# A diffusion transformer layer on one core: modulation dots one by one through the first feed-forward half, GpSimd making the rests of the plain quarter-weights, earlier residual loads, and the filters' small network moved ahead of stage two

## The chip, the cores and the metric

The kernel runs on one core of one Trainium2 chip. The metric is the device time of one execution in microseconds (us), and the time of a version is the median of its runs. TensorE (PE in the profile, PEld for its weight loads), VectorE (DVE), ScalarE (ACT), GpSimd (POOL) and SyncE (SP) each run their own list of instructions in order. Most transfers are issued on SP's queue, and a few on GpSimd's.

## What is computed

One layer on 512 latent tokens and 256 context tokens of width 1024, all in fp32. This is the reference, cut to what matters here:

```python
m  = jnp.split(silu(c) @ mod_w + mod_b, 9);  mc = jnp.split(silu(c_ctx) @ mod_w + mod_b, 9)
h  = half_ffn(h,  m[0],  m[1],  m[2],  ffn_w_gate[0], ffn_w_up[0], ffn_w_down[0])   # hidden width 2816
hc = half_ffn(hc, mc[0], mc[1], mc[2], ffn_w_gate[0], ffn_w_up[0], ffn_w_down[0])
n  = modulate(rms_norm(h), m[3], m[4]);  nc = modulate(rms_norm(hc), mc[3], mc[4])
s_fw, s_bw = context_states(nc, ...)
out = token_mixers(n, s_fw, s_bw, hyena_kernels(...), ...)    # n @ w_in; HGRN2 heads; Hyena by FFT
h  = h + m[5] * out
h  = half_ffn(h, m[6], m[7], m[8], ffn_w_gate[1], ffn_w_up[1], ffn_w_down[1])
return rms_norm(h) * final_norm_w
# half_ffn(h) = h + 0.5 * gate * ((silu(x @ wg) * (x @ wu)) @ wd),  x = modulate(rms_norm(h), shift, scale)
```

`hyena_kernels` runs a small network on 512 positions (33 to 64 to 64 values, each layer followed by a sine) and multiplies its result with `hyena_w3`; the filters come out of that.

## The kernel before

Every fp32 product is made as three TensorE products of parts. ScalarE rounds an operand to its high part (`whi`), VectorE subtracts that from the operand to get the rest (`wlo`, line 143), and `mm3` (lines 316 to 319) adds high x high, low x high and high x low in PSUM. So each weight costs ScalarE and VectorE an instruction each before TensorE can use it.

**First feed-forward half (`ffn0`).** The 22 hidden blocks of 128 are worked in five groups, of 4, 4, 4, 4 and 6 blocks. A group makes gate and up products and then its part of the down product, in eight column blocks of 128 (`dm`). The down product's partial results are accumulated in DRAM (`y_dram`, `yc_dram`) and read back in the last group. Group 0 uses the plain form. In groups 1 to 4, two blocks are made together by a seven-product scheme: `quads0` cuts the two blocks' weights into quarters and yields seven quarter-weights of 128x512, of which three are plain quarters (a11, a12, a22) and four are sums (`qs`, line 250); `pair_products0` runs seven products of 12 matmuls over 386 columns (`product0`) and combines them. There are 18 calls of `quads0`: nine pairs of blocks, each for gate and for up. The plain quarters' rests come from a negated copy by ScalarE and an accumulating DMA from DRAM on GpSimd's queue; the rests of the sums come from VectorE.

**The modulation (`mod_steps`)** is a generator beside this work. It has 56 steps; each takes one 512 KB row of `mod_w` (`wmod`, loaded one step ahead into two buffers) and VectorE multiplies it with `silu(c)` and `silu(c_ctx)` and sums (line 392). The first 24 steps have a latent dot in two halves of 512 and a context dot of 1024; the other 32 have one of 1024. `adv(bg, n)` takes n steps. It is called once per pair of blocks and with n = 2 after each of a group's eight down columns.

**The token mixer (stage two)** has work of two kinds. Chains (context norm, filters, the convolutions in four channel blocks, the four heads) hang on one engine after the other. `fill` tiles (`ps_w`, 52 of them, 24 matmuls of 512 columns for most) are projections of the normed latents that nothing holds up. `Clock.run` puts them between the steps of a chain, which sets the order on each engine. `allowed` says which tiles may be taken: the z tiles (decays and queries of a head) not before the convolutions have begun. In a convolution `ps_e` is the forward transform and `ps_i` the inverse one.

**Buffers.** Tiles come from rotating pools: `c8` has 12 buffers of 8 KB per partition, `c4` 8, `c2` 15, `c1` 6, `quarters` 2, `wraw` 3, and `whi` and `wlo` 3 each. A load waits on SP's queue until its buffer is free, and what stands behind it on the queue waits as well.

Of the kernel before, what the change touches and what calls it, by code (L numbers as in the profile page):

```python
# [20 lines left out]
L = 512  # L21
# [74 lines left out]
def layer_kernel(ctx: ExitStack, tc: tile.TileContext, a: dict, out: bass.AP):  # L96
# [38 lines left out]
    def load(dst, src):  # L135
        nc.sync.dma_start(out=dst, in_=src)
# [15 lines left out]
    for g, (f0, f1) in enumerate(GROUPS0):  # L152
        if g == 0:
            gu = [(a[w][0, ft], 1024) for ft in range(f0, f1) for w in ("wg", "wu")]
            plan += hold(gu[:6], [RING] * 3 + [ONE8, RES2, TWO4]) + gu[6:]
        else:
            plan += [(a[w][0, ft], a[w][0, ft + 1], QUAD0) for ft in range(f0, f1, 2) for w in ("wg", "wu")]
        down = [(a["wd"][0, dm, :, f0 * P:f1 * P], (f1 - f0) * P) for dm in range(KT)]
        plan += hold(down, [RING] * 3 + [ONE8] * 3 + [RING] * 2) + down[0:3] if g == len(GROUPS0) - 1 else down
# [20 lines left out]
    def allowed(f):  # L180
        if f[0] == "z":
            return state["conv"] and f[1] - state["heads"] < 3
        if f[0] == "pb":
            return ("z", 3, 1) in state["done"] and state["heads"] > 1
        return True
# [53 lines left out]
    def quads0(src0, src1):  # L239


        raws = []
        for src in (src0, src1):
            raws.append(raw_tile("wraw"))
            load(raws[-1], src)
        (a11, a12), (a21, a22) = (r.rearrange("p (h c) -> h p c", h=2) for r in raws)

        def total(x, y):
            t = c2("qs", [512])
            V.tensor_tensor(out=t, in0=x, in1=y, op=ALU.add)  # L250
# [407 lines left out]
    prefetch(6)  # L658
# [12 lines left out]
    def filter_net():  # L671
        mf = c8("mf", [896])
        load(mf, a["masks"])
# [23 lines left out]
        PE.matmul(p1[:64, :], zw[0:EMB, 512:576], zw[0:EMB, 0:512], start=True, stop=True)  # L697
        h1 = zw[0:64, 1024:1536]
# [5 lines left out]
        h2 = zw[:, 1536:2048]  # L704
# [168 lines left out]
    def product0(name, x):  # L873
        whi, wlo, _ = weights()
        p_ = ps(name)
        for k in range(4):
            ks = slice(k * P, k * P + P)
            mm3([p_[:, 0:HW]], whi[:, ks], wlo[:, ks], [x[k]], k == 0, k == 3)
        return p_[:, 0:HW - 1]

    def pair_products0(name):
# [5 lines left out]
        V.tensor_tensor(out=u2, in0=product0("ps_p6", tsum[1]), in1=p1, op=ALU.add)  # L887
        A.copy(p7, product0("ps_p7", tsum[2]))
# [4 lines left out]
        V.tensor_tensor(out=res[:, 0, 0], in0=product0("ps_p2", [xone(4 + k, 0) for k in range(4)]), in1=p1, op=ALU.add)  # L893
        V.scalar_tensor_tensor(out=res[:, 1, 0], in0=product0("ps_p4", tsum[3]), scalar=-1.0, in1=res[:, 1, 0],
# [13 lines left out]
    bg = mod_steps()  # L908

    def ffn0():  # L910
        for gi, (f0, f1) in enumerate(GROUPS0):
            ml, mc = [], []
            if gi == 0:
# [51 lines left out]
            else:  # L965
                for ft in range(f0, f1, 2):
# [4 lines left out]
                    adv(bg)  # L971
# [11 lines left out]
            if gi < len(GROUPS0) - 1:  # L983
                for dm in range(KT):
# [12 lines left out]
            def residual0(h_, x_src, y_src, p_, m, dm, al, n):
                x, y = al("xr", [n]), al("yr", [n])
                load(x, x_src)
                load(y, y_src)  # L1000
                V.tensor_tensor(out=y, in0=p_, in1=y, op=ALU.add)
                V.scalar_tensor_tensor(out=h_, in0=y, scalar=m[:, 16 + dm:17 + dm], in1=x, op0=ALU.mult, op1=ALU.add)
# [6 lines left out]
            hc2 = c8("hc", [KT, C])  # L1009
            nhi, nlo = (Halves([c8(x, [4, L], F32R) for _ in range(2)]) for x in ("nhi", "nlo"))  # L1010
            for dm in range(KT):
# [3 lines left out]
                residual0(hk(hl2, dm), x0_dram[:, dm], y_dram[:, dm], pl, m_lat, dm, c2, L)  # L1015
# [4 lines left out]
            for n, dm in enumerate((6, 7, 3, 4, 5, 0, 1, 2)):  # L1020
# [5 lines left out]
                residual0(hc2[:, dm], a["ctxT"][:, dm], yc_dram[:, dm], pc[:, 0:C], m_ctx, dm, c1, C)  # L1026
# [25 lines left out]
    def fill_tile(f):  # L1052
# [63 lines left out]
        elif kind == "z":  # L1116
# [619 lines left out]
```

## Time and profile before

| | |
|---|---|
| median of 3 runs | 1676.86 us (1676.05 to 1678.73) |
| the profiled execution's time | 1675.28 us |
| its span in the trace | 1673.5 us |
| mean granted TensorE clock | 0.939 of full speed |
| busy: TensorE, VectorE | 89%, 69% of the span |
| busy: ScalarE, GpSimd | 40%, 26% of the span |

The profiled execution lies 1.6 us below the median. An engine's busy share is a mean over stages in which different things set the pace; a gap of TensorE costs its own length and sometimes a lower granted clock around it.

### The profile page before, as it was taken

Reading aid. Unit: us, or ns where it says so; the run is one execution under the profiler, and the core shown is the slowest. Engines: PE = TensorE matmul, PEld = TensorE weight load, DVE = VectorE, ACT = ScalarE, POOL = GpSimd, SP = SyncE. Lnnn points to the kernel's source line nnn. Section 1 sums busy time; section 2 is a strip of 40 time slices with the busy share of each in tenths; the row PEclk is TensorE's granted clock in tenths of the full one; section 3 lists DMA queues with packets and bytes.
Section 4 is the critical chain, followed back from the end, with each engine's and each line's share of the span. In section 5 each row is a group of like instructions: output and inputs, shape, how many; then the busy total and the mean of one; then the engine's idle time right before and its main releaser. Section 6 shows DMA issues by size and latency. Waiting matters only on the chain.

```text
span 1673.5 us, 22809 instructions
## 1 busy us (share of the span) xinstructions
PE 1489.9 (89%) x8560; PEld 1328.3 (79%) x8560; DVE 1150.2 (69%) x1814; ACT 670.9 (40%) x1196; POOL 429.3 (26%) x353
## 2 busy tenths in 40 slices
PE   8697698998999977999999438998989899999997
PEld 5596697998989966777777437887769898989897
DVE  7777776766836756654355896777755776959687
ACT  5352343444546524443233112335333433535353
POOL 1320224334343300003667401211233010202120
PEclk9899798999999998999999768999899999999999
DMA  7417649869595563334355312113243223232323
GB/s 308 157 51 239 178 106 235 231 173 269 149 195 117 125 199 117 125 119 157 97 166 180 129 56 74 63 51 114 76 154 105 70 82 103 88 114 95 107 78 93
DMA packets 92751, 223.77 MB, mean 134 GB/s; under 512 B 10396, under 2 KB 25504, under 8 KB 92257
## 3 DMA queue, kind: packets, MB, share of 16 engines
q1 hardware_dynamic: 75024, 193.18, 35.3%
q0 software_dynamic: 16032, 27.93, 9.3%
q8 instruction: 67, 1.10, 0.3%
q10 hardware_dynamic: 1584, 1.20, 0.2%
q14 instruction: 44, 0.35, 0.1%
HBM read 190.04 MB, written 32.24 MB: 133 GB/s over the span
## 4 chain that ended last, share of the span: by engine, by line
PE 62%; DVE 17%; DMA 11%; issue 5%; ACT 2%; POOL 2%; SPq 0%; ACTq 0%; DVEq 0%; POOLq 0%
PE ps_p L319 6%; PE ps_p L316 6%; PE ps_p L317 6%; PE ps_w L316 5%; PE ps_w L317 5%; PE ps_w L319 5%; DMA wmod<-in_mod_w 4%; PE ps_dl L316 3%; PE ps_dl L317 3%; PE ps_dl L319 3%; DVE x L1225 2%; DVE wlo L143 1%; DVE wmod L392 1%; PE ps_s L1362 1%; DMA yr<-y_dram 1%
## 5 line engine op out<-in xcount | busy, mean ns | idle before, releaser
L142 ACT CAST whi<-wraw 128x1024 fp32r<-128x1024 f32 (+2 forms) x160 | 134.5, 842 | 297.3 <-issue 88.2
L143 DVE TENSOR_TENSOR wlo<-wraw,whi 128x1024 fp32r<-128x1024 f32 (+2 forms) x111 | 114.1, 1031 | 88.6 <-ACT whi L142 86.5
L316 PE MATMUL ps_w<-nhi,whi 128*128 128x512 f32 x352 | 144.9, 412 | 0.0
L319 PE MATMUL ps_w<-nhi,wlo 128*128 128x512 f32 x352 | 141.0, 401 | 2.4 <-DVE wlo L143 2.4
L317 PE MATMUL ps_w<-nlo,whi 128*128 128x512 f32 x352 | 141.8, 403 | 0.0
L317 PE MATMUL ps_dl<-mid,whi 128*128 128x512 f32 (+1 forms) x318 | 122.5, 386 | 0.0
L319 PE MATMUL ps_dl<-mid,wlo 128*128 128x512 f32 (+1 forms) x318 | 122.2, 386 | 0.0
L316 PE MATMUL ps_dl<-mid,whi 128*128 128x512 f32 (+1 forms) x318 | 121.2, 388 | 0.0
L143 POOL TENSOR_TENSOR wlo<-wraw,whi 128x1024 fp32r<-128x1024 f32 x22 | 53.9, 2450 | 242.1 <-ACT whi L142 150.6
L1562 POOL TENSOR_TENSOR u<-p,res 128x512 f32<-128x512 f32 x18 | 33.0, 1832 | 284.5 <-ACT p L1557 140.8
L392 DVE SCALAR_TENSOR_TENSOR wmod<-wmod,cvb 128x1024 f32<-128x1024 f32 x56 | 68.6, 1229 | 31.4 <-DMA wmod<-in_mod_w 31.0
L316 PEld LDWEIGHTS ps_w<-nhi,whi 128*128 128x128 f32 x352 | 68.4, 194 | 17.1 <-issue 1.6
L319 PEld LDWEIGHTS ps_w<-nhi,wlo 128*128 128x128 f32 x352 | 67.9, 193 | 15.4 <-DVE wlo L143 2.8
L317 PEld LDWEIGHTS ps_w<-nlo,whi 128*128 128x128 f32 x352 | 68.2, 194 | 11.6
L142 ACT CAST wlo<-qs 128x512 fp32r<-128x512 f32 x72 | 43.7, 621 | 81.0 <-DVE qs L250 56.3
L319 PE MATMUL ps_p<-bh,whi 128*128 128x386 f32 x180 | 63.5, 354 | 8.9 <-DMA whi<-in_wg 5.7
L142 ACT CAST whi<-qs 128x512 fp32r<-128x512 f32 x72 | 44.1, 620 | 63.8 <-DVE qs L250 24.4
L316 PEld LDWEIGHTS ps_dl<-mid,whi 128*128 128x128 f32 x318 | 59.6, 188 | 11.8 <-ACT mid L142 0.2
L319 PEld LDWEIGHTS ps_dl<-mid,wlo 128*128 128x128 f32 x318 | 60.0, 189 | 7.1
L317 PEld LDWEIGHTS ps_dl<-mid,whi 128*128 128x128 f32 x318 | 59.8, 188 | 7.1
L143 DVE TENSOR_TENSOR wlo<-qs,wlo 128x512 fp32r<-128x512 f32 x72 | 54.9, 773 | 11.8 <-ACT wlo L142 11.5
L319 PE MATMUL ps_p<-bh,wlo 128*128 128x386 f32 x180 | 61.9, 344 | 1.1 <-DMA wlo<-in_wg 1.0
(541 smaller groups left out, 4923.7 us busy)
## 6 DMA issues: line engine op xcount, KB each, us to landing
wmod<-in_mod_w SPq DMA_DIRECT2D x56, 512.0 KB, 6.0
wraw<-in_wg SPq DMA_DIRECT2D x44, 512.0 KB, 4.1
wraw<-in_wu SPq DMA_DIRECT2D x44, 512.0 KB, 4.7
wraw<-in_w_in SPq DMA_DIRECT2D x44, 512.0 KB, 3.5
wraw<-in_wd SPq DMA_DIRECT2D x35, 384.0 KB, 3.6
wraw<-in_wd SPq DMA_DIRECT2D x40, 256.0 KB, 3.0
wm<-in_mod_w SPq DMA_DIRECT2D x16, 512.0 KB, 9.0
y_dram<-yt POOLq DMA_DIRECT2D x24, 256.0 KB, 8.1
```

The costliest lines, as they stand in the source:

```text
L142: A.copy(hi, x)
L143: return eng.tensor_tensor(out=lo, in0=x, in1=hi.bitcast(F32), op=ALU.subtract)
L316: PE.matmul(o, whi, xhi, start=first, stop=False)
L317: PE.matmul(o, whi, xlo, start=False, stop=False)
L319: PE.matmul(o, wlo, xhi, start=False, stop=last)
L392: return V.scalar_tensor_tensor(out=out_, in0=raw, scalar=1.0, in1=vec, op0=ALU.mult, op1=ALU.mult, accum_out=res)
L1225: V.tensor_tensor(out=r, in0=x, in1=y, op=op)
L1362: PE.matmul(p_[:, ss], km[:, ss], view(QA, c * P, ([2 * b, P // (2 * b)], [L + b, 2], [1, b])), start=True, stop=True)
L1562: G.tensor_tensor(out=u57, in0=p57, in1=res[:, 1:2].broadcast_to([P, 2, 256]), op=ALU.add)
```

## The change

The change has nine edits. (1) `adv(bg)` is called four times per pair of blocks (inside `pair_products0`) and once per down column, where it was once per pair and twice per column; so steps move from the downs into the products. (2) In `quads0` the rests of the three plain quarters are subtracted by GpSimd: 54 subtractions of 128x512 take the place of 54 negated copies on ScalarE and 54 accumulating DMAs. (3) `product0` fetches three weights ahead and not two. (4) In `residual0` of the last group, x and y of all column blocks are read at once into `c8` tiles ahead of the last down product, not per block through `c2` and `c1`. (5) `filter_net` runs behind `mod_steps` in the same background generator, with two `c4` tiles, and no longer at the start of `filters`. (6) Context norm and filters run as two chains side by side over the fill, and `forward_table` comes ahead of both. (7) Head 0's z tiles are allowed before the convolutions. (8) In `shifts`, at the start, the latent dots are made in two halves, and four of the eight rows are loaded ahead of the sixth kept weight. (9) Of the last down's kept weights one lies in a `quarters` buffer, not in `c8`.

```diff
@ plan, allowed
-        plan += hold(down, [RING] * 3 + [ONE8] * 3 + [RING] * 2) + down[0:3] if ...
+        plan += hold(down, [RING] * 3 + [ONE8] * 2 + [RES2] + [RING] * 2) + down[0:3] if ...
-            return state["conv"] and f[1] - state["heads"] < 3
+            return f[1] == 0 or (state["conv"] and f[1] - state["heads"] < 3)
@ quads0
-            if src is None:
-                split(t[:, 0], t[:, 1], x)
-            else:
-                A.copy(t[:, 0], x)
-                A.activation(t[:, 1], t[:, 0].bitcast(F32), AF.Copy, scale=-1.0)
-                nc.gpsimd.dma_start(out=t[:, 1], in_=src, accum_op=ALU.add)
+            split(t[:, 0], t[:, 1], x, eng)
-        yield both(a11, src0[:, 0:512])
+        yield both(a11, G)
...
-        yield both(a12, src0[:, 512:1024])
-        yield both(a22, src1[:, 512:1024])
+        yield both(a12, G)
+        yield both(a22, G)
@ shifts and its loads
-            dot(junk, shift_w[kt], cvb[0], m0[:, kt, 0:1])
+            junk = c2("junk", [512])
+            for h, res in enumerate((m0[:, kt, 0:1], m_part[:, kt:kt + 1])):
+                hs = slice(512 * h, 512 * h + 512)
+                dot(junk, shift_w[kt][:, hs], cvb[0][:, hs], res)
...
-    shift_w = rows(range(KT), "wm0")
+    shift_w = rows(range(4), "wm0")
+    prefetch(6)
+    shift_w += rows(range(4, KT), "wm0")
@ product0, pair_products0
-        whi, wlo, _ = weights()
+        whi, wlo, _ = weights(3)
...
         V.tensor_tensor(out=u2, in0=product0("ps_p6", tsum[1]), in1=p1, op=ALU.add)
+        adv(bg)
...
+        adv(bg)
@ ffn0
-                    adv(bg)
                     u_ = pair_products0("u")
...
-                    adv(bg, 2)
+                    adv(bg)
...
+            yl = [c8("yl", [4, L]) for _ in range(2)]
+            hc2, yc = (c8(x, [KT, C]) for x in ("hc", "yc"))
+            for dm in range(0, KT, 2):
+                i, ks = dm // 4, slice(dm % 4, dm % 4 + 2)
+                load(hl2[i][:, ks], x0_dram[:, dm:dm + 2])
+                load(yl[i][:, ks], y_dram[:, dm:dm + 2])
+            load(hc2, a["ctxT"])
+            load(yc, yc_dram)
@ background, filters, stage two
+    def background():
+        yield from mod_steps()
+        yield from filter_net()
...
-    ck.run([context_norm()], fill, lambda i: True)
     ftab = forward_table()
-    ck.run([filters()], fill, lambda i: True)
+    ck.run([context_norm(), filters()], fill, lambda i: True, 2)
```

How the instructions stand then, at three places. First VectorE between group 0's down product and group 1's first sum of quarters, in the kernel before: the last rows ahead of the first `qs`.

```order
L392 SCALAR_TENSOR_TENSOR wmod,m_ctx<-wmod,cvb 128x1024
L392 SCALAR_TENSOR_TENSOR junk,m_lat<-wmod,cvb 128x512
L392 SCALAR_TENSOR_TENSOR junk,m_part<-wmod,cvb 128x512
L392 SCALAR_TENSOR_TENSOR wmod,m_ctx<-wmod,cvb 128x1024
L392 SCALAR_TENSOR_TENSOR junk,m_lat<-wmod,cvb 128x512
L392 SCALAR_TENSOR_TENSOR junk,m_part<-wmod,cvb 128x512
L392 SCALAR_TENSOR_TENSOR wmod,m_ctx<-wmod,cvb 128x1024
L392 SCALAR_TENSOR_TENSOR junk,m_lat<-wmod,cvb 128x512
L250 TENSOR_TENSOR qs<-wraw 128x512
```

In the changed kernel the rows ahead of the same first `qs` are these (the dots' line is 386 there; `wlo<-wraw,whi` is the rest of a down weight).

```order
L143 TENSOR_TENSOR wlo<-wraw,whi 128x512
L386 SCALAR_TENSOR_TENSOR junk,m_part<-wmod,cvb 128x512
L386 SCALAR_TENSOR_TENSOR wmod,m_ctx<-wmod,cvb 128x1024
L386 SCALAR_TENSOR_TENSOR junk,m_lat<-wmod,cvb 128x512
L143 TENSOR_TENSOR wlo<-wraw,whi 128x512
L386 SCALAR_TENSOR_TENSOR junk,m_part<-wmod,cvb 128x512
L386 SCALAR_TENSOR_TENSOR wmod,m_ctx<-wmod,cvb 128x1024
L386 SCALAR_TENSOR_TENSOR junk,m_lat<-wmod,cvb 128x512
L386 SCALAR_TENSOR_TENSOR junk,m_part<-wmod,cvb 128x512
L386 SCALAR_TENSOR_TENSOR wmod,m_ctx<-wmod,cvb 128x1024
L386 SCALAR_TENSOR_TENSOR junk,m_lat<-wmod,cvb 128x512
L249 TENSOR_TENSOR qs<-wraw 128x512
```

The down weights' rests now stand among the dots up to shortly before the first `qs`, where before the last rows were dots alone; and 6 1/3 steps stand between the first dot and the first `qs`, where it was 13 1/3.

Second, TensorE in the first channel block of the convolutions, before: the inverse transform's first two matmuls stand right behind the forward transform's.

```order
L319 MATMUL ps_e<-zhi,ft 128x256
L316 MATMUL ps_e<-zhi,ft 128x256
L317 MATMUL ps_e<-zlo,ft 128x256
L319 MATMUL ps_e<-zhi,ft 128x256
L316 MATMUL ps_i<-ys,it 128x256 x2
L316 MATMUL ps_e<-zhi,ft 128x256
```

After: the same place, where five `ps_w` tiles stand between the two. The last of them ends here.

```order
L311 MATMUL ps_w<-nlo,whi 128x512
L313 MATMUL ps_w<-nhi,wlo 128x512
L310 MATMUL ps_w<-nhi,whi 128x512
L311 MATMUL ps_w<-nlo,whi 128x512
L313 MATMUL ps_w<-nhi,wlo 128x512
L310 MATMUL ps_i<-ys,it 128x256
L311 MATMUL ps_i<-ys,it 128x256
```

Ten such tiles, five and five, are now in the first two channel blocks; none was there before, and in the last two blocks there is none in either kernel.

Third, SP's queue around the last group's down product, before. `xr` and `yr` are a column block's residual and partial result, `wd` the down weights.

```order
L136 DMA wraw<-in_wd 128x768 x6
L136 DMA xr<-x_dram 128x512
L136 DMA yr<-y_dram 128x512
L139 DMA h_dram<-hl 128x512
L136 DMA xr<-x_dram 128x512
L136 DMA yr<-y_dram 128x512
L136 DMA wraw<-in_wd 128x768 x3
```

After:

```order
L136 DMA hl<-x_dram 128x1024
L136 DMA yl<-y_dram 128x1024
L136 DMA hl<-x_dram 128x1024
L136 DMA yl<-y_dram 128x1024
L136 DMA hl<-x_dram 128x1024
L136 DMA yl<-y_dram 128x1024
L136 DMA hl<-x_dram 128x1024
L136 DMA yl<-y_dram 128x1024
L136 DMA wraw<-in_wd 128x768
L136 DMA hc<-in_ctxT 128x2048
L136 DMA yc<-yc_dram 128x2048
L136 DMA wraw<-in_wd 128x768 x3
```

Before, the loads of x and y came block by block, the second pair behind the first store of `h_dram`; now the eight loads shown, of 512 KB each, stand behind the third down weight, two of 1 MB behind the fourth, and the stores of `h_dram` come after all of them.

## Rows read from the trace of the kernel before

**Rows 1.** The page: busy time, share of the span and instructions of each engine.
```profile
PE 1489.9 (89%) x8560; PEld 1328.3 (79%) x8560; DVE 1150.2 (69%) x1814; ACT 670.9 (40%) x1196; POOL 429.3 (26%) x353
```

**Rows 2.** TensorE's waits: us in total, times, longest.
```profile
PE ps_i L316 <- ACT ys L142: 40.4, 4, 22.2
PE ps_p L316 <- ACT wlo L142: 26.3, 4, 21.6
PE ps_sum L459 <- DVE acc L451: 20.6, 4, 13.4
```

**Rows 3.** Windows: us; PE, PEld, DVE, ACT, POOL busy; granted clock; DMA share; GB/s.
```profile
119.80:153.50 33.70, 33.70 (x194) 29.43 (x193) 25.29 (x57) 12.07 (x27) 0.91 (x1) 1.00 0.73 234
153.50:242.70 89.20, 64.05 (x339) 61.83 (x338) 68.23 (x135) 36.91 (x69) 22.77 (x23) 0.85 0.63 165
276.30:352.40 76.10, 66.79 (x340) 64.46 (x339) 57.67 (x100) 35.09 (x67) 25.67 (x26) 0.89 0.79 208
385.70:454.10 68.40, 62.83 (x338) 60.72 (x337) 52.10 (x80) 34.95 (x67) 25.37 (x25) 0.95 0.80 210
487.80:580.50 92.70, 89.97 (x507) 88.68 (x506) 59.43 (x86) 53.90 (x99) 36.24 (x37) 1.00 0.61 131
580.50:654.00 73.50, 57.22 (x317) 50.54 (x315) 43.84 (x65) 24.70 (x40) 3.58 (x2) 0.88 0.49 154
654.00:696.00 42.00, 34.38 (x138) 28.00 (x139) 25.60 (x47) 14.69 (x27) 0.00 (x0) 0.88 0.38 125
696.00:928.40 232.40, 232.40 (x1052) 182.00 (x1051) 119.78 (x137) 83.64 (x120) 103.75 (x95) 1.00 0.44 146
928.40:980.90 52.50, 12.08 (x76) 11.08 (x75) 49.49 (x82) 9.19 (x15) 14.67 (x13) 0.62 0.31 104
```

**Rows 4.** VectorE's dots, 153.5 to 242.7 us: busy us, mean ns, idle before.
```profile
L392 DVE SCALAR_TENSOR_TENSOR junk<-wmod,cvb 128x512 f32<-128x512 f32 x22 | 15.2, 690 | 3.7 <-DMA wmod<-in_mod_w 3.3
L392 DVE SCALAR_TENSOR_TENSOR wmod<-wmod,cvb 128x1024 f32<-128x1024 f32 x12 | 14.7, 1224 | 0.3
L392 DVE DVE_READ_ACCUMULATOR junk<-wmod,cvb 128x1 f32 x22 | 1.8, 83 | 0.0
```

**Rows 5.** Timeline of VectorE, then TensorE: start us, us, instruction [idle before].
```profile
127.89 0.68 DVE L392 SCALAR_TENSOR_TENSOR junk<-wmod,cvb 128x512 f32<-128x512 f32 x1
...
174.99 0.69 DVE L250 TENSOR_TENSOR qs<-wraw 128x512 f32<-128x512 f32 x1
...
177.60 0.69 PE L316 MATMUL ps_p<-tt,wlo 128*128 128x386 f32 x1 [21.62 <-ACT wlo L142]
```

**Rows 6.** VectorE's sums of quarters in group 4: busy us, mean ns, idle before.
```profile
L250 DVE TENSOR_TENSOR qs<-wraw 128x512 f32<-128x512 f32 x10 | 10.1, 1008 | 4.3 <-DMA wraw<-in_wu 4.3
L250 DVE TENSOR_TENSOR qs<-qs,wraw 128x512 f32<-128x512 f32 x5 | 7.2, 1431 | 0.2
L250 DVE TENSOR_TENSOR qs<-wraw,qs 128x512 f32<-128x512 f32 x6 | 4.1, 682 | 0.0
```

**Rows 7.** GpSimd, line 809: min/median/max ns, first and last start.
```profile
L809 POOL TENSOR_TENSOR te<-te x4: 1303/1523/2260, 798.5 to 930.5; 128x512 f32<-128x512 f32 x4
```

**Rows 8.** Timeline of TensorE in the last down product.
```profile
581.15 0.40 PE L316 MATMUL ps_dl<-mid,whi 128*128 128x512 f32 x1
581.38 0.39 PE L317 MATMUL ps_dl<-mid,whi 128*128 128x512 f32 x1
```

**Rows 9.** Timeline around the end of the last down's latent part.
```profile
631.26 1.87 PE L459 MATMUL ps_sum<-pick,acc 128*128 128x4 f32 x8 [13.42 <-DVE acc L451]
...
634.38 0.69 DVE L1001 TENSOR_TENSOR yr<-ps_dl,yr 128x512 f32<-128x512 f32 x1 [3.17 <-DMA yr<-y_dram]
```

**Rows 10.** Timeline of VectorE at the start, a shift dot.
```profile
50.23 1.22 DVE L392 SCALAR_TENSOR_TENSOR junk<-wm,cvb 128x1024 f32<-128x1024 f32 x1 [4.03 <-DMA wm<-in_mod_w]
```

**Rows 11.** The filter network's first operation, two layers: ns, starts.
```profile
L688 DVE TENSOR_SCALAR uk<-ps_f,sm x2: 794/798/802, 728.3 to 741.1; 64x512 f32<-64x512 f32 x1, 128x512 f32<-128x512 f32 x1
```

**Rows 12.** VectorE's rests of fill weights, 696.0 to 928.4 us.
```profile
L143 DVE TENSOR_TENSOR wlo<-wraw,whi 128x1024 fp32r<-128x1024 f32 x29 | 37.7, 1301 | 55.8 <-ACT whi L142 55.8
```

More of the change, by code (lines that the diff above doesn't have):

```diff
@@ L158, in layer_kernel @@
         down = [(a["wd"][0, dm, :, f0 * P:f1 * P], (f1 - f0) * P) for dm in range(KT)]
-        plan += hold(down, [RING] * 3 + [ONE8] * 3 + [RING] * 2) + down[0:3] if g == len(GROUPS0) - 1 else down
+        plan += hold(down, [RING] * 3 + [ONE8] * 2 + [RES2] + [RING] * 2) + down[0:3] if g == len(GROUPS0) - 1 else down
     plan += [None] * 52
@@ L251, in total, with both @@
             return t
-        def both(x, src=None):
+        def both(x, eng=V):
             w = ("whi", "wlo")[wstate["slot"]]
@@ L657, in layer_kernel @@
         first_norm(kt, 0, hl, rl[0], LATS, c2)
-    prefetch(6)
+    prefetch(5)
     cvb = [c4("cvb", [D]) for _ in range(2)]
@@ L661, in layer_kernel @@
         load(cvb[i], a["cvec"][:, i * D:i * D + D].partition_broadcast(P))
-    junk = c4("junk", [1024])
-    V.memset(junk[:, 0:1], 0.0)
-    shift_w = rows(range(KT), "wm0")
+    shift_w = rows(range(4), "wm0")
+    prefetch(6)
+    shift_w += rows(range(4, KT), "wm0")
     for i in range(2):
@@ L671, in filter_net @@
     def filter_net():
-        mf = c8("mf", [896])
-        load(mf, a["masks"])
+        za, zb = (c4("zw", [1024]) for _ in range(2))
+        load(za[:, 0:896], a["masks"])
         sm64 = c1("sm64", [132])
@@ L676, in filter_net @@
         yield
-        V.tensor_copy(masks.rearrange("p l s -> p (l s)"), mf)
+        V.tensor_copy(masks.rearrange("p l s -> p (l s)"), za[:, 0:896])
         yield
-        zw = c8("zw", [2048])
-        load(zw[0:EMB, 0:512], a["zT"])
-        load(zw[0:EMB, 512:576], a["hy_w1"])
+        load(za[0:EMB, 0:512], a["zT"])
+        load(za[0:EMB, 512:576], a["hy_w1"])
         yield
-        uk = c8("uk", [2, 512])
         def sine_layer(n, dst, p_, b, fr):
-            u, kk = uk[0:n, 0], uk[0:n, 1]
+            u, kk = za[0:n, 0:512], za[0:n, 512:1024]
             V.tensor_scalar(out=u, in0=p_[0:n, :], scalar1=b[0:n], scalar2=fr[0:n], op0=ALU.add, op1=ALU.mult)
@@ L696, in filter_net @@
         p1 = ps("ps_f1")
-        PE.matmul(p1[:64, :], zw[0:EMB, 512:576], zw[0:EMB, 0:512], start=True, stop=True)
-        h1 = zw[0:64, 1024:1536]
+        PE.matmul(p1[:64, :], za[0:EMB, 512:576], za[0:EMB, 0:512], start=True, stop=True)
+        h1 = zb[0:64, 0:512]
         sine_layer(64, h1, p1, sm64[:, 128:129], sm64[:, 129:130])
@@ L703, in filter_net @@
         PE.matmul(p2, sm64[0:64, 0:128], h1, start=True, stop=True)
-        h2 = zw[:, 1536:2048]
+        h2 = zb[:, 512:1024]
         sine_layer(P, h2, p2, sm64[:, 130:131], sm64[:, 131:132])
@@ L731, in filters @@
     def filters():
-        for _ in filter_net():
-            yield 0.4, 3.0
         worder = [(hh, q) for hh in range(2) for _ in range(2) for q in range(4)]
@@ L907, in layer_kernel @@
     n_c = 2 * (HC + 2)
-    bg = mod_steps()
+    def background():
+        yield from mod_steps()
+        yield from filter_net()
+    bg = background()
     def ffn0():
@@ L932, in ffn0 @@
                     first_norm(kt, 1, hc, rx[0], CTXS, c1)
+                V.tensor_tensor(out=m0[:, :, 0], in0=m0[:, :, 0], in1=m_part, op=ALU.add)
                 V.tensor_tensor(out=m0, in0=m0, in1=sm[:, S_MODB:S_MODB + KT].unsqueeze(2).broadcast_to([P, KT, 2]), op=ALU.add)
@@ L993, in ffn0, with residual0 @@
                             nc.gpsimd.dma_start(out=y[:, dm], in_=t, accum_op=ALU.add)
-                    adv(bg, 2)
+                    adv(bg)
                 continue
[L997 to L1000, printed above, removed]
+            def residual0(h_, y, p_, m, dm):
                 V.tensor_tensor(out=y, in0=p_, in1=y, op=ALU.add)
-                V.scalar_tensor_tensor(out=h_, in0=y, scalar=m[:, 16 + dm:17 + dm], in1=x, op0=ALU.mult, op1=ALU.add)
+                V.scalar_tensor_tensor(out=h_, in0=y, scalar=m[:, 16 + dm:17 + dm], in1=h_, op0=ALU.mult, op1=ALU.add)
             for _ in bg:
@@ L1008, in ffn0 @@
             hl2 = [c8("hl", [4, L]) for _ in range(2)]
-            hc2 = c8("hc", [KT, C])
+            yl = [c8("yl", [4, L]) for _ in range(2)]
[6 more added lines that the diff above has]
+            load(yc, yc_dram)
             nhi, nlo = (Halves([c8(x, [4, L], F32R) for _ in range(2)]) for x in ("nhi", "nlo"))
@@ L1014, in ffn0 @@
                 down(kept[dm], lx, [pl])
-                residual0(hk(hl2, dm), x0_dram[:, dm], y_dram[:, dm], pl, m_lat, dm, c2, L)
+                residual0(hk(hl2, dm), hk(yl, dm), pl, m_lat, dm)
                 sq_add(acc, hk(hl2, dm), dm, c2, L)
@@ L1025, in ffn0 @@
                     adv(nl, 1 if n < 3 else 2)
-                residual0(hc2[:, dm], a["ctxT"][:, dm], yc_dram[:, dm], pc[:, 0:C], m_ctx, dm, c1, C)
+                residual0(hc2[:, dm], yc[:, dm], pc[:, 0:C], m_ctx, dm)
                 sq_add(accc, hc2[:, dm], n, c1, C)
@@ L1124, in fill_tile @@
                 if d == 0:
-                    hs["F"] = c8("F", [2, T])
-                    hs["KR"] = c8("KR", [2, T])
+                    for k in ("F", "KR"):
+                        hs[k] = c8(k, [2, T]) if hd else \
+                            quarters(k).rearrange("p a b -> p (a b)")[:, 0:2 * T].rearrange("p (d t) -> p d t", d=2)
                 ci = slice(d * NH + hd, d * NH + hd + 1)
```

## The prediction, made before the changed kernel had run

> **What bounds the kernel now.** I read the page first. TensorE is busy for 1489.9 us of the span and VectorE for 1150.2 [rows 1], so what can be won is mostly TensorE's idle time, some 184 us, and what a lowered clock costs around it. The second view is TensorE's waits. The three that lead the list [rows 2] are the inverse transform waiting for its spectrum (40.4 us in four waits), a quarter-weight in the product stages (26.3, of which one wait is 21.6) and the sum of squares of the first half's result (20.6, of which one is 13.4). Each lies in one stage, so the third view is windows by stage [rows 3]. In their order they are group 0's down product, the products of groups 1, 2, 3 and 4, the last down product (latents, then context), the context norm, the filters with the fill, and the first two channel blocks of the convolutions.
>
> What the reader is to see there: group 0's down and the filters have TensorE busy throughout, so there only less TensorE work helps. Group 4 makes three pairs of blocks and no modulation dots in 92.7 us with TensorE busy for 89.97 at full clock: 30.9 us a pair. Groups 1 to 3 make two pairs each, which at that pace is 61.8, and take 89.2, 76.1 and 68.4, at granted clocks of 0.85, 0.89 and 0.95. The first two convolution blocks take 52.5 us with 12.08 of TensorE, at 0.62, while VectorE is busy for 49.49.
>
> **The change, term by term**, against the profiled execution's 1675.3 us, 1.6 below the median.
>
> *Product stages (edits 1, 2, 3).* A modulation step of the first kind costs VectorE two dots at 0.690, one at 1.224 and three reads of 0.083 us [rows 4], together 2.85; a later one 1.31. The first dot starts at 127.89 and group 1's first sum of quarters at 174.99; 13 1/3 steps stand between. TensorE, having waited 21.62 us, gets its first product at 177.60 [rows 5]. Now 6 1/3 steps stand there: 7 steps of 2.85 are 20 us of VectorE's queue, nearly the wait. They move behind that sum, into products. Is VectorE late there? Without dots, group 4 asks 59.43 / 3 = 19.8 us a pair of it [rows 3], so 39.6 for two pairs. Group 1's products now hold eight steps (22.8), those of groups 2 and 3 eight short ones (10.5).
>
> The rests come on top. No row shows GpSimd making one, but it makes sums of the same 128x512 tiles in 1.3 us at best and 1.523 in the median [rows 7]: I take 1.5. What does that take from VectorE? In group 4 its sums of two loaded quarters take 0.682 us undisturbed in one form, 1.008 and 1.431 in the others [rows 6], which is 7 us over 21 sums, and the rests of the sums lose some 2 us more. GpSimd was busy for 36.24 us there [rows 3], of which its DMA issues are about 16, so 20 with sums. That is 9.4 / 20, or 0.47 us lost per us of GpSimd's sums. A group of two pairs has 12 rests: 12 x 1.5 x 0.47 = 8.4 us. The bounds are nothing lost and the whole 1.5 us a rest.
>
> VectorE then needs 39.6 + 22.8 + 8.4 = 70.8 us in group 1 and 58.5 in groups 2 and 3, against TensorE's 61.8. I take 74 (VectorE's work and some waits), 64 and 64 (TensorE's pace and some waits). In group 4 VectorE has 59.4 + 12.6 + 7.5, under 92.7, so I take 93. The 7.5 is the filter network: two layers of six operations whose dearest takes 0.798 us [rows 11], so under 10 in any case. The sum is 295 against 326.4: **31 less**. Best case: no interference, 45 less (62, 62, 62 and 92.7 are 279, and a little of the downs). Worst case: the whole 1.5 us a rest (80, 68, 68 and 96 are 312, so 14 less) and 10 us of new waits: 4 less. The 54 copies on ScalarE and the accumulating DMAs that go cost nothing now, as ScalarE is busy for half or less of each window. The downs stay as they are: group 0's is TensorE's own 33.70, and one step a column leaves VectorE less work there, not more.
>
> The Trainium skill (SBUF — State Buffer, section "SBUF: two separate sides") speaks against edit 2: the port pair that VectorE and GpSimd share is an exclusive lock, so a VectorE operation with two SBUF inputs and a GpSimd operation that reads SBUF shut each other out for a whole instruction. By it each rest would take its full 1.5 us of VectorE, and the stages would come to 80 + 68 + 68 + 96 = 312, 14 less and not 31. The trace agrees in part: sums in SBUF take up to 1.431 where 0.682 would do [rows 6], but not each one.
>
> *Last down and context norm (edits 4, 9).* The down stage takes 73.5 us. A matmul of 512 columns starts every 0.23 us [rows 8]; 8 columns x 6 blocks x 3 of them are 33, and the context's, at half the columns, 17: TensorE's own part is 50. The last waits there are a y load that VectorE waits 3.17 us for and, behind it, a sum for which TensorE stood 13.42 us [rows 9]. The loads now go out before the down begins: 6 MB at the 234 GB/s of the fastest window [rows 3] are 26 us, and they can start some 8 us before the stage, when the buffers of the up product's operand sums come free (its last four products, 48 matmuls, follow). Behind them on SP wait four down weights, needed from 12 us into the stage on; the first latent columns may wait a little. Fill starts where the down ends, and edit 6 lets it start at once beside the norm. I put TensorE's restart at 55 us and not 73.5, and save 4 of the norm's own gaps: **22 less**. Bounds: 12 (the loads are late as before, only the sum's wait goes) and 27.
>
> *Filters and convolutions (edits 5, 6, 7).* Ten fill tiles move from the filters' stage into the first two convolution blocks. Each is 24 matmuls of 0.23, so 5.5 us. The filter stage is TensorE's own time throughout [rows 3], so it loses 55 us. Each tile also needs its weight's rest, 1.3 us of VectorE [rows 12]. In the convolution blocks TensorE then has 55 + 11, VectorE 49.5 + 13 = 62.5: I take 68.5 in place of 52.5, 16 more. **39 less**. Bounds: 25 (the two engines half in turn, 82.5) and 45 (VectorE's sum alone, with no wait). The last two blocks keep their waits, since no fill stands there.
>
> *Start (edit 8).* VectorE waits 4.03 us for a row before its first dots [rows 10]; half of the rows now go ahead of a 512 KB weight. Eight dots in halves cost 8 x (2 x 0.773 - 1.307) = 1.9 us more. **3 less**; bounds 6 less and 2 more.
>
> Sum: 31 + 22 + 39 + 3 = 95, so 1580 for the profiled execution and **1582** for the median.
>
> **The rivals.** *A, the products gain nothing:* VectorE loses so much to GpSimd that all 31 go, 0.58 us a rest beyond my price. For it speak the 1.431 in [rows 6], against it that TensorE has some slack in groups 2 to 4: 1613. By the page's lock alone it would be 1599. *B, the filters become the bound:* with 55 us of fill gone, norm and filters hold 209 us of TensorE work (232.4, and about 32 of the norm's 34.38 at full clock, less 55), but VectorE's 119.8 - 7.5 + 25.6 and GpSimd's 103.75 [rows 3] add to 242 if they run strictly in turn. Then 33 come back: 1615. Against it: GpSimd's sums of one filter can lie under VectorE's work on the next. *C, the early loads come late*, because the `c8` buffers come free late or the down weights queue behind 6 MB: the term falls to 4, and it ends at 1600. *D, slower:* GpSimd runs in order. A rest may stand behind a combining sum that waits for a later product, and TensorE, which needs that rest, waits in turn. From 95 / 54 = 1.8 us a rest it decides against the change; with 1.5 for the rest itself and 1.3 for one sum ahead of it, 2.8 each is 151 us: 1733. Against it: weights are now made three ahead.
>
> **How the numbers follow.** Forecast 0.62 (own range 1562 to 1600), A 0.14, B 0.12, C 0.05, D 0.04, and 0.03 for more gain than the bounds or no change at all. The range takes in A, B and C above, with some us of scatter, and reaches down to about where all the best bounds together would end (45 + 27 + 45 + 6 = 123 less, 1554): 1556 to 1622. It leaves out D and the tails. Within 0.2% is about what a measurement of this kernel can tell from no change; all cases but D and part of the last give faster: 0.94, same 0.02, slower 0.04.
>
> **What would show it.** Right: TensorE's gap before group 1 falls from 21.6 us to a few, groups 1 to 3 take about 74, 64 and 64 at a granted clock near 1, the wait for `acc` goes, `ps_w` matmuls fill the first two convolution blocks, and VectorE's 128x512 sums get longer. Wrong: GpSimd leads TensorE's waits in the products (A, D), TensorE idles among the filters (B), or VectorE waits for `yl` (C). I would be furthest off if a weight that now comes later on SP's queue held TensorE.

## The result and the profile after

The changed kernel takes 1597.85 us in the median (1596.63 to 1599.40, four runs), beside 1676.45 for the kernel before: a ratio of 0.9529, 95% interval 0.9513 to 0.9546. That is 78.6 us less, where 95 were forecast. The page of its profile begins so:

```profile
span 1597.4 us, 22680 instructions
...
PE 1473.6 (92%) x8560; PEld 1312.8 (82%) x8560; DVE 1190.6 (75%) x1833; ACT 634.5 (40%) x1141; POOL 473.4 (30%) x350
```

TensorE is busy for 16 us less than before [rows 1], so some 60 of the 76 us that the span lost were idle time. VectorE is busy for 40 us more, although hardly any of its work is new (the start's dots are made in halves). TensorE's waits (us in total, times, longest):

```profile
PE ps_j L310 <- ACT ys L142: 22.1, 3, 13.9
PE ps_gc L310 <- ACT bh L142: 18.2, 1, 18.2
PE ps_ot L1439 <- ACT on L1433: 11.6, 4, 3.2
PE ps_p L310 <- ACT wlo L142: 11.0, 1, 11.0
PE ps_p L313 <- DVE wlo L143: 8.4, 10, 1.4
PE ps_p L313 <- DVE whi L143: 7.1, 6, 2.3
PE ps_p L310 <- ACT whi L142: 6.6, 3, 2.8
```

Of the three waits that led before [rows 2], `ps_i` and `ps_sum` are gone from the top and the 21.6 us ahead of group 1 too. In the products four smaller ones stand in their place, 33.1 us together, one of them 11.0, and the start's wait has grown to 18.2. The windows by stage, with columns as in [rows 3], are in their order group 0's down, the products of groups 1 to 4, the last down, context norm and filters together, the first two convolution blocks, and the rest up to the projections behind the heads.

```profile
125.40:159.20 33.80, 33.80 (x195) 29.54 (x194) 27.11 (x59) 12.57 (x29) 1.30 (x1) 1.00 0.75 253
159.20:229.30 70.10, 61.32 (x338) 58.77 (x337) 70.00 (x108) 28.05 (x56) 34.98 (x23) 1.00 0.38 122
...
264.00:342.80 78.80, 63.38 (x339) 60.59 (x338) 70.67 (x103) 27.98 (x56) 36.29 (x25) 0.94 0.46 140
...
376.50:440.90 64.40, 61.46 (x338) 60.61 (x337) 56.16 (x73) 28.38 (x56) 36.97 (x25) 0.97 0.51 155
...
474.60:570.50 95.90, 93.11 (x510) 90.73 (x509) 79.65 (x110) 46.59 (x88) 49.45 (x38) 0.98 0.34 102
570.50:624.40 53.90, 53.48 (x314) 46.99 (x313) 40.43 (x61) 24.17 (x38) 2.76 (x2) 1.00 0.59 215
624.40:856.30 231.90, 226.64 (x1057) 179.98 (x1056) 136.78 (x173) 85.29 (x131) 95.85 (x92) 0.99 0.42 138
856.30:922.80 66.50, 66.50 (x326) 55.80 (x325) 60.01 (x91) 24.06 (x35) 18.08 (x15) 1.00 0.47 155
922.80:1149.80 227.00, 182.34 (x1113) 163.47 (x1111) 168.76 (x296) 85.84 (x173) 45.89 (x19) 0.90 0.26 89
```

Against the kernel before, by the spans of the two profiled executions (76.1 us in all): group 0's down begins 5.6 later; from there to the last down it is 460.7 before and 445.1 now, 15.6 less; last down, norm and filters take 347.9 and 285.8, 62.1 less; the first two convolution blocks 52.5 and 66.5, 14 more; blocks three and four and the heads 245.2 and 227.0, 18.2 less; the rest is the same within 0.2.

### The profile page after: what moved, and what is told of

Same layout as the page of the kernel before. It is cut to its first block, busy times and chain, and to the rows that moved or that the text cites. A ratio compares the mean times of both kernels' runs of the same rounds, so it can differ in the third digit from the quotient of the medians.

```text
span 1597.4 us, 22680 instructions
## 1 busy us (share of the span) xinstructions
PE 1473.6 (92%) x8560; PEld 1312.8 (82%) x8560; DVE 1190.6 (75%) x1833; ACT 634.5 (40%) x1141; POOL 473.4 (30%) x350
## 4 chain that ended last, share of the span: by engine, by line
PE 59%; DVE 22%; DMA 7%; issue 6%; ACT 3%; POOL 1%; SPq 0%; ACTq 0%; DVEq 0%; POOLq 0%
PE ps_w L310 5%; PE ps_w L313 5%; PE ps_w L311 5%; PE ps_p L313 4%; PE ps_p L310 4%; PE ps_p L311 4%; PE ps_dl L310 3%; PE ps_dl L311 3%; PE ps_dl L313 3%; DMA wmod<-in_mod_w 3%; DVE wlo L143 2%; DVE junk L386 2%; DVE wmod L386 2%; DVE qs L249 2%; DVE whi L143 2%
## 5 line engine op out<-in xcount | busy, mean ns | idle before, releaser
L142 ACT CAST whi<-wraw 128x512 fp32r<-128x512 f32 (+2 forms) x187 | 151.4, 810 | 299.1 <-issue 78.4
L143 DVE TENSOR_TENSOR wlo<-wraw,whi 128x1024 fp32r<-128x1024 f32 (+2 forms) x114 | 124.6, 1095 | 57.4 <-ACT whi L142 55.1
L386 DVE SCALAR_TENSOR_TENSOR wmod<-wmod,cvb 128x1024 f32<-128x1024 f32 x56 | 73.5, 1313 | 24.6 <-DMA wmod<-in_mod_w 24.3
L311 PEld LDWEIGHTS ps_w<-nlo,whi 128*128 128x128 f32 x352 | 67.2, 191 | 11.5
L142 ACT CAST whi<-qs 128x512 fp32r<-128x512 f32 x72 | 44.3, 619 | 78.8 <-DVE qs L249 40.2
L143 DVE TENSOR_TENSOR whi<-qs,whi 128x512 fp32r<-128x512 f32 x72 | 67.4, 947 | 4.6 <-ACT whi L142 4.3
L143 DVE TENSOR_TENSOR wlo<-qs,wlo 128x512 fp32r<-128x512 f32 x72 | 58.1, 813 | 16.6 <-ACT wlo L142 15.9
L143 POOL TENSOR_TENSOR wlo<-wraw,wlo 128x512 fp32r<-128x512 f32 x27 | 48.2, 1785 | 65.7 <-ACT wlo L142 58.3
```

The lines of the kernel that those rows point to most:

```text
L311: PE.matmul(o, whi, xlo, start=False, stop=False)
L386: return V.scalar_tensor_tensor(out=out_, in0=raw, scalar=1.0, in1=vec, op0=ALU.mult, op1=ALU.mult, accum_out=res)
```

## Experiments

The theory after this result: the stages of the mixer and the last down did what the prediction says, and the 16 us that are missing lie in the products, where GpSimd's rests (edit 2) take VectorE time just where the steps (edit 1) have been put, and at the start (edit 8). The rival: the rests are cheap, and the rows of `mod_w` or the pairs' weights are late. Every run was compared with runs of the kernel before on the same chip; the ratios are to that kernel, so 0.9529 is the changed kernel.

**1. The rests by copies and accumulating DMAs again (edit 2 undone): 1585.05 us, 0.9457 (0.9435 to 0.9479).**

```diff
-            split(t[:, 0], t[:, 1], x, eng)
+            if src is None:
+                split(t[:, 0], t[:, 1], x)
+            else:
+                A.copy(t[:, 0], x)
+                A.activation(t[:, 1], t[:, 0].bitcast(F32), AF.Copy, scale=-1.0)
+                nc.gpsimd.dma_start(out=t[:, 1], in_=src, accum_op=ALU.add)
...
-        yield both(a11, G)
+        yield both(a11, src0[:, 0:512])
...
```

> The changed kernel with edit 2 undone: the 54 rests come again from a negated copy on ScalarE and an accumulating DMA. If GpSimd's rests cost VectorE time that TensorE waits for (my price, 8.4 us a group, with group 1's VectorE now busy for 70.00 of 70.1 us), groups 1 and 2 get 6 to 8 us shorter each and the time is about 1585. If the rests are free and the accumulating DMAs are late beside the rows of mod_w, TensorE waits for them in the products and it is 1605 or more. Group 1's VectorE busy time tells which.

Windows of groups 1 and 2 in this run, and the wait that came back:

```profile
158.90:220.40 61.50, 60.08 (x338) 59.01 (x337) 59.95 (x109) 33.91 (x65) 25.42 (x23) 1.00 0.72 192
...
254.10:328.60 74.50, 64.63 (x338) 62.96 (x337) 59.19 (x108) 35.51 (x67) 25.70 (x25) 0.89 0.78 199
```

```profile
PE ps_p L318 <- DMA whi<-in_wg: 14.1, 4, 5.2
```

Edit 2 alone costs 13 us. Group 1's VectorE is busy for 59.95 us and not 70.00, and the stage takes 61.5 us and not 70.1; group 2 gains less than I expected, 4.3 us. The rival's wait for accumulating DMAs is there too (14.1 us), so this is not yet the best place for the rests. From group 0's down to the end of group 4's products (125 to 560 us) VectorE makes the same 573 instructions as in the changed kernel, whose line stands in the next experiment, in

```profile
125.00:560.00 435.00, 414.96 (x2290) 392.00 (x2289) 322.71 (x573) 210.80 (x410) 155.42 (x156) 0.97 0.76 201
```

322.71 us, where the changed kernel takes 366.08: 43.4 us more beside GpSimd's 54 rests, or 0.80 each.

**2. The rests on VectorE: 1569.20 us, 0.9358 (0.9339 to 0.9377).**

```diff
-        yield both(a11, G)
+        yield both(a11)
...
-        yield both(a12, G)
-        yield both(a22, G)
+        yield both(a12)
+        yield both(a22)
```

> The changed kernel with the 54 rests subtracted by VectorE itself (0.69 us each undisturbed, 8.3 us a group of two pairs), GpSimd with none. On GpSimd they cost VectorE 42 us of busy time over groups 1 to 4 against the run with accumulating DMAs, 0.78 us a rest. If that is what a rest costs wherever it runs, VectorE's busy time and the 1598 stay within 4 us. If GpSimd's part in the exclusion is worse than the work itself, it is 1590; if VectorE is so full that its own 37 us of work decide, 1605.

It is faster than any case that was named: 28.7 us less than the changed kernel. VectorE's groups in the changed kernel, from group 0's down to the end of group 4's products (125 to 571 us; busy us, mean ns, idle before):

```profile
L386 DVE SCALAR_TENSOR_TENSOR wmod<-wmod,cvb 128x1024 f32<-128x1024 f32 x56 | 73.5, 1313 | 24.6 <-DMA wmod<-in_mod_w 24.3
L143 DVE TENSOR_TENSOR whi<-qs,whi 128x512 fp32r<-128x512 f32 x36 | 43.3, 1214 | 2.1 <-ACT whi L142 1.9
...
L249 DVE TENSOR_TENSOR qs<-wraw 128x512 f32<-128x512 f32 x36 | 39.6, 1101 | 4.5 <-DMA wraw<-in_wg 4.1 <-DMA wraw<-in_wu 0.5
```

and with the rests on VectorE (125 to 545 us, the same work):

```profile
L249 DVE TENSOR_TENSOR qs<-wraw 128x512 f32<-128x512 f32 x36 | 31.3, 871 | 5.5 <-DMA wraw<-in_wu 3.8 <-DMA wraw<-in_wg 1.6
L143 DVE TENSOR_TENSOR whi<-qs,whi 128x512 fp32r<-128x512 f32 x36 | 29.9, 841 | 0.7 <-ACT whi L142 0.5
...
L143 DVE TENSOR_TENSOR whi<-wraw,whi 128x512 fp32r<-128x512 f32 x27 | 20.1, 743 | 2.0 <-ACT whi L142 2.0
L143 DVE TENSOR_TENSOR wlo<-wraw,wlo 128x512 fp32r<-128x512 f32 x27 | 19.1, 709 | 0.8 <-ACT wlo L142 0.7
```

The same 36 rests of sums take 1.214 us on average beside GpSimd's rests and 0.841 without them. Over the two stretches (windows of 125 to 571 and 125 to 545 us) VectorE is busy for

```profile
125.00:571.00 446.00, 415.62 (x2291) 389.25 (x2291) 366.08 (x573) 176.43 (x356) 200.87 (x157) 0.98 0.54 161
```

```profile
125.00:545.00 420.00, 410.50 (x2292) 388.63 (x2291) 356.80 (x627) 179.05 (x356) 117.33 (x103) 0.98 0.59 174
```

366.08 us where it does not make the 54 rests, and 356.80 where it does, of which they are 20.1 + 19.1 = 39.2. GpSimd spent 89.4 us on them in the changed kernel (1.66 each):

```profile
L143 POOL TENSOR_TENSOR wlo<-wraw,wlo 128x512 fp32r<-128x512 f32 x27 | 48.2, 1785 | 65.7 <-ACT wlo L142 58.3 <-DVE whi L143 3.7 <-DVE wmod L386 3.1
L143 POOL TENSOR_TENSOR whi<-wraw,whi 128x512 fp32r<-128x512 f32 x27 | 41.2, 1527 | 74.3 <-ACT whi L142 70.3 <-DVE wlo L143 2.9 <-DVE qs L249 1.1
```

So VectorE's other work took 317.6 without GpSimd's rests and 366.1 beside them: 48.5 us lost, 0.90 a rest. Handing the rests to GpSimd took more of VectorE's time than making them. The stretch is 26 us shorter, more than those 9. By the two lines above TensorE's idle time in it fell from 30.4 us to 9.5, and its busy time by 5; its waits for `ps_p` in the list after the result fell from 33.1 us to 12.9 (7.5, 3.6 and 1.8). Group 3 then runs like this:

```profile
359.80:419.00 59.20, 59.20 (x338) 59.20 (x338) 54.17 (x83) 27.65 (x54) 17.79 (x14) 1.00 0.55 165
```

TensorE is busy throughout, and two pairs take 59.2 us, less than the 61.8 that the prediction took as TensorE's pace. The four product stages together take 283.6 us in this run (63.7, 69.3, 59.2 and 91.4), 42.8 less than before the change: near the 45 that the prediction named for no interference at all, although VectorE makes all the rests here.

**3. The steps as before the change (edit 1 undone), with the rests on GpSimd and on VectorE: 1609.32 us, 0.9593 (0.9571 to 0.9615), and 1599.74, 0.9528 (0.9496 to 0.9559).**

```diff
         V.tensor_tensor(out=u2, in0=product0("ps_p6", tsum[1]), in1=p1, op=ALU.add)
-        adv(bg)
...
-        adv(bg)
...
+                    adv(bg)
                     u_ = pair_products0("u")
...
-                    adv(bg)
+                    adv(bg, 2)
```

> The changed kernel with edit 1 undone: one step per pair of blocks, two per down column. If the queue of dots ahead of group 1's first sum is what made the wait, a gap of some 20 us is back there and groups 1 to 3 take 15 to 20 us more: 1615. If the gain came from GpSimd's rests and the third weight ahead, the time stays within 5 us of 1598.

> Rests on VectorE and the steps as before the change (edit 1 undone). With the rests on GpSimd, spreading the steps gave only 11 us. If GpSimd's rests took the rest of that gain away, spreading gives more here, some 20 us: 1589. If spreading is worth 11 wherever the rests are, 1580.

TensorE's first wait in the second of these runs is the old one:

```profile
PE ps_p L310 <- ACT wlo L142: 29.5, 3, 22.7
```

In the first run that wait is back as well (21.6 us). Spreading the steps is worth 11.5 us beside GpSimd's rests and 30.5 without them: the two edits draw on the same VectorE time.

**4. Where group 2's 11.0 us come from: six steps in group 1's down product: 1592.88 us, 0.9505 (0.9476 to 0.9533).**

```diff
-                    adv(bg)
+                    if gi != 1 or dm < 6:
+                        adv(bg)
```

> The changed kernel with six steps in place of eight in group 1's down product (the other two come later). TensorE waits 11.0 us at the start of group 2; VectorE's list has dots that wait for rows ahead of the first sum. If those dots make the wait, two fewer of them, 4.2 us apart, bring it to about 3 and the time to 1591. If the wait is for the pair's weights, it stays at 11 and the time at 1598.

The timeline of the changed kernel at that place shows VectorE's waits for rows, the first sum, and then TensorE:

```profile
264.86 0.69 DVE L386 SCALAR_TENSOR_TENSOR junk<-wmod,cvb 128x512 f32<-128x512 f32 x1 [1.93 <-DMA wmod<-in_mod_w]
...
269.80 0.69 DVE L386 SCALAR_TENSOR_TENSOR junk<-wmod,cvb 128x512 f32<-128x512 f32 x1 [2.24 <-DMA wmod<-in_mod_w]
...
274.04 0.69 DVE L386 SCALAR_TENSOR_TENSOR junk<-wmod,cvb 128x512 f32<-128x512 f32 x1 [1.54 <-DMA wmod<-in_mod_w]
...
274.66 0.69 DVE L249 TENSOR_TENSOR qs<-wraw 128x512 f32<-128x512 f32 x1
...
277.26 0.69 PE L310 MATMUL ps_p<-tt,wlo 128*128 128x386 f32 x1 [11.00 <-ACT wlo L142]
```

The pair's weights had been issued at 245.7 and 254.3 us and take 8 to land; ahead of the sum on VectorE stand dots that wait for rows, one row every 4 to 5 us. With two steps fewer the wait fell to 6.6 us, by one row's pace and not by two, and group 2's stage from 78.8 to 73.4. The dots ahead of the sum make the wait; how many of them stand there is not simply the steps taken. By the medians this is 5 us, but the intervals of the two kernels overlap.

**5. The start: all eight rows behind the sixth kept weight again: 1589.72 us, 0.9478 (0.9453 to 0.9502).**

```diff
-    prefetch(5)
+    prefetch(6)
...
-    shift_w = rows(range(4), "wm0")
-    prefetch(6)
-    shift_w += rows(range(4, KT), "wm0")
+    shift_w = rows(range(KT), "wm0")
```

> The changed kernel with only the loading order of edit 8 undone (all eight rows behind the sixth kept weight; the dots stay in halves). In the changed kernel the context's sum of squares stands further back among TensorE's products, ScalarE gets it 5.9 us later, and silu(c) and the dots follow. If that order costs the start its time, the sum comes early again and the gap before the first context product falls from 18.2 to about 13: 1593. If the dots in halves cost it, meeting GpSimd's products at 2.9 us each, the time stays at 1598.

ScalarE at the start of the changed kernel, and in this run:

```profile
51.13 0.26 ACT L459 ACTIVATE rr<-ps_sum,eps_t 128x2 f32<-128x2 f32 x1 [10.00 <-PE ps_sum L453]
```

```profile
45.07 0.26 ACT L459 ACTIVATE rr<-ps_sum,eps_t 128x2 f32<-128x2 f32 x1 [4.52 <-PE ps_sum L453]
```

In the changed kernel the rows land in time, but `silu(c)`, which the dots need, stands on ScalarE's list behind this reciprocal root, and that behind a sum of squares ahead of which TensorE has 66 matmuls of the first products, where it had 47 before. The first context product waits 18.2 us and in this run 11.3. Dots that meet GpSimd's products take four times as long in both (2.74 to 2.89 us, see the last section), so what the expectation says of them is real, but it isn't what the order changed: with the halves kept, group 0's down begins here at 118.2 us, earlier than the 119.8 of the kernel before.

Not all of the changed kernel's 5.6 us at the start belong to edit 8. From 20 to 33 us, ahead of any product, the mean granted clock of its profiled execution is 0.87, and 1.00 before the change; 16 matmuls of `ps_m` take 8.7 us there, where they took 7.0.

```profile
20.00:33.00 13.00, 11.86 (x36) 3.55 (x34) 9.23 (x15) 5.76 (x12) 0.00 (x0) 0.87 1.02 412
```

In both runs of experiment 3, which start as the changed kernel does, that clock is 1.00 and group 0's down begins at 123.6 and 123.7 us. So edit 8 costs 3.8 there and the clock 1.7; why the clock is lower in some runs and not in others stays open.

**6. The last down's loads per block again (edits 4 and 9 undone): 1626.21 us, 0.9690 (0.9673 to 0.9707).**

```diff
...
-            for dm in range(0, KT, 2):
-                load(hl2[i][:, ks], x0_dram[:, dm:dm + 2])
-                load(yl[i][:, ks], y_dram[:, dm:dm + 2])
-            load(hc2, a["ctxT"])
-            load(yc, yc_dram)
...
+                x, y = al("xr", [n]), al("yr", [n])
+                load(x, x_src)
+                load(y, y_src)
...
```

> The changed kernel with edits 4 and 9 undone: x and y again block by block through c2 and c1. If the late loads made the waits of the last down product, the gap of some 13 us before the sum is back, the stage takes 70 us and not 53.9, fill starts that much later, and the time is 1618 to 1626. If the stage gained from edit 5 and the order of the chains only, it stays at 1598.

The stage's window in this run, and the wait for the sum on TensorE:

```profile
570.00:648.20 78.20, 58.71 (x316) 52.46 (x314) 43.12 (x64) 24.14 (x38) 3.31 (x2) 0.85 0.45 141
```

```profile
623.71 1.44 PE L453 MATMUL ps_sum<-pick,acc 128*128 128x4 f32 x6 [16.28 <-DVE acc L445]
```

The early loads are worth 28.4 us; in the changed kernel the stage takes 53.9 at full clock.

**7. Head 0's z tiles (edit 7 undone): 1615.15 us, 0.9619 (0.9598 to 0.9640); the chains one after the other (edit 6 undone): 1594.15, 0.9495 (0.9479 to 0.9512).**

```diff
-            return f[1] == 0 or (state["conv"] and f[1] - state["heads"] < 3)
+            return state["conv"] and f[1] - state["heads"] < 3
...
```

```diff
+    ck.run([context_norm()], fill, lambda i: True)
     ftab = forward_table()
-    ck.run([context_norm(), filters()], fill, lambda i: True, 2)
+    ck.run([filters()], fill, lambda i: True)
```

> The changed kernel with edit 7 undone. In its order 6.4 fill tiles stand in the first two convolution blocks and not 10.2, and 3.6 more stand ahead of the first head. By my price of a tile (5.5 us of TensorE, 1.3 of VectorE in the block) the second block gets about 6 us shorter and what follows 20 longer: 1612. If the heads have TensorE time to spare for these tiles, it stays at 1598.

> The changed kernel with only edit 6 undone: context norm first, then forward_table, then the filters. In its order 8.4 tiles stand in the first two blocks and not 10.2. If running the two chains side by side is what gives the filters' stage its fill early, TensorE gets gaps in the norm and the time is 1608. If the tiles alone count, 1.8 tiles of 5.5 us come back elsewhere at full price or less: 1598 to 1605.

(The first edit also gives head 0's `F` and `KR` tiles back their `c8` buffers; that part was not tried by itself.) TensorE's waits in the first of these, the second and third in its list, and in the second run the second in its list:

```profile
PE ps_i L310 <- ACT ys L142: 16.7, 2, 16.1
PE ps_j L310 <- ACT ys L142: 16.7, 3, 9.1
```

```profile
PE ps_j L310 <- ACT ys L142: 16.9, 3, 8.9
```

Edit 7 is worth 17 us: without it the second block has 16.1 us of its old wait, and three tiles stand again behind the second block. Edit 6 is worth nothing here, or costs some 4: with it the filters' stage is 3.4 us shorter and 1.8 more tiles stand in the second block, but the third block's transform waits 13.9 us in place of 8.9. That the tiles cause this longer wait is likely and not shown.

**8. What the experiments point to, together.** The rests on VectorE and the start's old order, with six steps in group 1's down product: 1565.23 us, 0.9317 (0.9290 to 0.9344). The same with edit 6 undone: **1562.21, 0.9298 (0.9271 to 0.9325)**, the fastest here. With edit 6 undone but eight steps: 1567.34, 0.9336 (0.9321 to 0.9350).

> The changed kernel with the rests on VectorE, the rows of the start behind the sixth kept weight, and six steps in group 1's down product. Alone these took 29, 8 and 5 us off. If they lie in different places, 42 together less what two of them share at group 2's start (its gap is 7.5 us with the rests on VectorE): 1557 to 1561. If the start's gain is lost later, 1566.

> The same and, besides, context norm and filters one after the other. Alone that took 4 us off. If it comes from the third and fourth convolution blocks, where a wait of 13.9 us became 8.9, it adds up: 1553 to 1557. If it came from the products' scatter, as the run before.

> Rests on VectorE, the start's rows behind the sixth kept weight, and norm and filters one after the other, with all eight steps in group 1's down product. With the rests on VectorE, group 2's first wait fell to 3.5 us by taking two steps out, but groups 1 to 3 each took 0.7 to 0.9 us more. If taking steps out of that down product gains nothing once the rests are off GpSimd, this is at 1558 to 1562, no slower than with six steps; if it does gain, 1565.

The gains do not add up: 37 to 41 us were expected of the first and 32.6 came, 4.0 more than with the rests on VectorE alone, whose interval overlaps. By the two profiles group 0's products end 5.3 us earlier than in run 2, groups 1 to 3 give back 2.4 of it and what follows 0.8; group 2's first wait is 3.5 us and not 7.5, but the steps that were moved cost its products as much. The last run speaks for keeping six steps, against my expectation that they gain nothing; the three intervals overlap, so the order among them stays open.

## Why the prediction was right or wrong

Sign and range held, and of the 95 us 78.6 came. That the sum came so near is in part luck: by the profiled executions the products with the downs between them missed by 15.4 and the start by 8.6, and the stages from the last down to the heads gave 5.3 more than forecast. By its own steps:

- **Product stages, forecast 31 less, measured 17.2 (309.2 us for 326.4): about half.** Group 1 (70.1 for 74), group 3 (64.4 for 64) and group 4 (95.9 for 93) were near; group 2 took 78.8 for 64, which is the whole of the miss. The step that failed is "those of groups 2 and 3 eight short ones (10.5)". In group 2's window stand ten half dots of the first kind and eleven dots of 1024:

```profile
L386 DVE SCALAR_TENSOR_TENSOR wmod<-wmod,cvb 128x1024 f32<-128x1024 f32 x11 | 14.5, 1318 | 0.1
...
L386 DVE SCALAR_TENSOR_TENSOR junk<-wmod,cvb 128x512 f32<-128x512 f32 x10 | 7.5, 751 | 5.8 <-DMA wmod<-in_mod_w 5.7
```

  With their reads they are 23.7 us of VectorE, since steps of group 1's down product, where a row comes only every 4 to 5 us, slid into this window; VectorE needed 70.67 us there and not 58.5. The price of a rest was nearly right: a rest took GpSimd 1.66 us and not 1.5, and cost VectorE 0.80 against the accumulating DMAs, where the sum had 0.70 (0.49 us per us of GpSimd for 0.47). Unpriced was the cheap alternative, the rests on VectorE.
- **Last down and norm, 22 less: right in mechanism.** The down stage takes 53.9 us and not 73.5, 19.6 less, of which the sum had 18.5. Undoing it costs 28.4, just beyond the bound of 27.
- **Filters and convolutions, 39 less: right in the sum, wrong in the place.** I took all ten tiles (55 us) from the filters' stage. In the order of instructions some seven left it and three left the stretch ahead of the heads. Norm and filters take 42.5 less, the first two blocks 14 more (16 forecast), and what follows 18.2 less, where I had nothing.
- **Start, 3 less: wrong, 5.6 more, of which 3.8 come from the edit.** I counted VectorE's wait for the row and not that `silu(c)` waits behind the context's sum, which moved back on TensorE's list. I argued from the loads where the chain went through TensorE and ScalarE.

One reading of [rows 6] was loose: only its first line is of sums of two loaded quarters, the other two add a loaded quarter to a sum. The price does not hang on it.

Rival A (the products gain nothing) came about half way, and its mechanism, VectorE's time lost to GpSimd's rests, is shown by experiments 1 and 2: edit 2 costs 13 us against the accumulating DMAs and 29 against VectorE. Rivals B, C and D did not come: TensorE is busy for 226.64 of 231.90 us in norm and filters, no wait for `yl` is among VectorE's first, and GpSimd is not among TensorE's.

The rule of the Trainium skill (SBUF — State Buffer, "SBUF: two separate sides") that I set against edit 2, 14 less for the products and not 31, comes near the measured 17.2, but not by its own sum: by a full lock a rest costs VectorE its whole 1.66 us, and the runs show 0.80 to 0.90 on average. What makes the difference no run shows; part of GpSimd's time may fall beside operations that do not meet it. Its direction was right.

## What to carry to other kernels

Before work is handed from one engine to another to relieve it, price what it takes from the first engine while both run; here 0.73 us of work (39.2 us for 54 rests) became 0.90 us of loss. Two edits that spend the same engine's slack in the same stretch can't be added: spreading the dots was worth 30 us or 11, depending on the other. And when a load is moved forward, follow what the consumer really waits for last; it may be another engine's in-order list.

## What was not expected of the hardware

A VectorE dot of 128x512 that starts while GpSimd multiplies 128x1024 takes 2.89 us where the dot before it took 0.69. This is the timeline at the start of the changed kernel, VectorE and then GpSimd.

```profile
58.14 0.69 DVE L386 SCALAR_TENSOR_TENSOR junk<-wm,cvb 128x512 f32<-128x512 f32 x1
...
58.75 2.89 DVE L386 SCALAR_TENSOR_TENSOR junk<-wm,cvb 128x512 f32<-128x512 f32 x1
...
58.44 5.45 POOL L612 TENSOR_TENSOR wm<-wm,cvb 128x1024 f32<-128x1024 f32 x2 [45.08 <-DVE junk L386]
```

GpSimd's two products take 2.7 us each, so the first ends near 61.2 us (an estimate, half of 5.45) and the dot at 61.6; the next dot, beside the second product, takes 2.87. So here the one engine stands still for the rest of the other's instruction.
